# A state space input stored as four wide DRAM writes, and three weight splits moved from VectorE to GpSimd, in a hybrid decoder step

## The chip, the core and the metric

The kernel runs on one core of a Trainium2 chip. A core has a matrix engine (TensorE, called PE in the profile; its weight loads are listed as PEld), three engines for elementwise work (VectorE or DVE, ScalarE or ACT, GpSimd or POOL), and a sequencer (SyncE or SP) whose queue issues the DMA transfers here. Each engine works through its own instructions in order and waits for the others by semaphores. The metric is the device time of one execution in microseconds (us); lower is better.

## What is computed

One layer of a hybrid decoder runs over a prompt of 2048 tokens and 32 sample tokens. Of the input projection `proj = rmsnorm(x) @ w_in` the first 768 columns are q, k, v of a sliding-window attention and the last 512 are `u`, the input of a diagonal state space model (S5) with 32 groups of 16 channels:

```python
q = proj[..., :ATTN_WIDTH]; k = ...; v = ...
u = proj[..., ATTN_WIDTH + 2 * KV_WIDTH:]
attn, k_win, v_win = attend(q, k, v, sinks)
ssm, h_re, h_im = _s5(u, h0_re, h0_im, ...)     # x[t] = a x[t-1] + B u[t];  y[t] = Re(C x[t]) + D u[t]
ssm = gelu(ssm); ssm = ssm * sigmoid(ssm @ w_glu + b_glu)
x = x + concat(rmsnorm(attn), rmsnorm(ssm)) @ w_out
x = x + conv_ffn(rmsnorm(x))
```

The outputs are the two token groups after a final rmsnorm, the last window of keys and values, the last S5 states and the last convolution rows.

## The kernel before

**Split products.** Every large matrix product is made from three: a weight is split into a high part (a rounded copy, made on ACT at L83) and a low part (the raw weight less the high part, L84, on an engine that the caller names), the activations likewise, and `mm3` (L89 to L91) adds high x high, high x low and low x high. `load_split_w` does this for the weights: a DMA into a raw tile (L146), then `split`. The raw tiles share two buffers, so a third raw tile is loaded only when the low part of the first has been made.

**First pass, u.** Tokens are taken in eight tiles (the first of 288 columns, the others of 256). For each, PE makes four products of 128 features (`u`), and DVE scales each into `uperm[m]` (L763), a tile of 128 partitions x 8 steps x 272 columns: partition 16 g + h is channel h of group g of feature tile m, time is cut into 8 steps within a column. Beside this pass DVE and POOL compute the tables of the state space model (`s5_params`): powers of the step factor, `bb1` and `bb2`, and two tables of phases, `fine` and `coarse`, on POOL.

**Between the passes.** The three tiles 1, 2, 3 of q weights are split with the low part on DVE (L781); the loads of token tile 1 follow (`prep2(1)`); then `uperm` goes to the DRAM scratch `uscr[group, 128, 272]`, one store for each of 32 groups (L787), in which 16 partitions are written so that row 16 s + h of a group holds step s of channel h.

**Second pass.** An order written out by hand (`ORDER`) mixes the generators: `q` is one of six 128-column products of a token tile (in the order v, k, then q 0 to 3), `a0` a step of attention block 0, `s0` a step of state space pair 0. It begins `s0 q q q q q q s0 q q s0 q s1 a0 ...`. PE follows this order strictly. The instructions of the other engines and of SP's queue are placed by a planner, which takes what is ready by its own model of time and, among what is ready, what comes first in the program; `tc.high_priority(offset=n)` moves a block n places forward in that precedence. A product is cleared from one of two PSUM buffers by DVE (L879 for q, L886 for k and v) into `f`, which has two buffers too; the low part of q is made on POOL, that of k on DVE (L84), and the `kp` tiles are zeroed (L830 to L837) and copied (L900) on POOL.

**A state space pair** (`s5_pair`) loads `u` for two groups from `uscr` (L385); DVE builds `vv`, an operator whose rows are (s, h) (L393 to L395), and `cl`; PE transposes `vv` (L403) and multiplies `cl` (L405) into `pk`; ACT copies that into `wk`; eight small DMAs place shifted copies of a 16-row piece into `tp`, 16 partitions each (L418). The next step multiplies `wk` with `u` (`pre`, `pim`, L442), DVE scans, and the last one multiplies `tp` with `u` and `cl` with the states into the output, which goes to `yscr`.

Of the kernel before, what the change touches and what calls it, by code (L numbers as in the profile page):

```python
# [9 lines left out]
F32 = mybir.dt.float32  # L10
# [3 lines left out]
ALU = mybir.AluOpType  # L14
# [4 lines left out]
P = 128  # L19
# [6 lines left out]
KD = D // P  # L26
# [36 lines left out]
HPD = 90  # L63
# [17 lines left out]
def split(nc, hi, lo, src, hi_eng, lo_eng):  # L81

    i = nc.scalar.copy(hi, src) if hi_eng is nc.scalar else hi_eng.tensor_copy(hi, src)  # L83
    return i.ins, lo_eng.tensor_tensor(lo, src, hi.bitcast(F32), ALU.subtract).ins  # L84
# [52 lines left out]
def load_split_w(c, pool, raw_pool, src, nk, cols, nm, lo_eng=None, hi_eng=None):  # L137

    nc = c.nc
    v = src.rearrange("(k p) n -> p k n", p=P)  # L140
    out = {}
    for m in cols:
        hi = pool.tile([P, nk, P], F32R, tag=f"{nm}h{m}", name=f"{nm}h{m}")
        lo = pool.tile([P, nk, P], F32R, tag=f"{nm}l{m}", name=f"{nm}l{m}")
        raw = raw_pool.tile([P, KD, P], F32, tag="wur", name=f"{nm}raw{m}")[:, 0:nk]
        nc.sync.dma_start(raw, v[:, :, m * P : m * P + P])  # L146
        split(nc, hi, lo, raw, hi_eng or nc.scalar, lo_eng or nc.gpsimd)
        out[m] = (hi, lo)
    return out
# [229 lines left out]
def s5_pair(c, pool, ps, gp, uscr, yscr):  # L379

    nc, v, gq = c.nc, c.nc.vector, c.nc.gpsimd
    gs = slice(2 * gp, 2 * gp + 2)
    nm = f"s{gp}"
# [3 lines left out]

    cl = pool.tile([P, 2, 9, 16], F32, tag="cl", name=f"cl_{nm}", bufs=2)
    ct = pool.tile([P, 2, 9, 16], F32, tag="ct", name=f"ct_{nm}")
    vv = pool.tile([P, 2, 8, 16], F32, tag="vv", name=f"vv_{nm}")  # L390
    pw = lambda x, n: x[:, gs, 0:n].unsqueeze(3).broadcast_to((P, 2, n, 16))
    hb = lambda x, n: x[:, gs, :].unsqueeze(2).broadcast_to((P, 2, n, 16))
    v.tensor_tensor(vv, pw(c.prv[0], 8), hb(c.bb1, 8), ALU.mult)  # L393
    v.tensor_tensor(ct[:, :, 0:8], pw(c.prv[1], 8), hb(c.bb2, 8), ALU.mult)
    v.tensor_tensor(vv, vv, ct[:, :, 0:8], ALU.add)  # L395
    v.tensor_tensor(cl, pw(c.pr, 9), hb(c.sc1, 9), ALU.mult)
    v.tensor_tensor(ct, pw(c.pi, 9), hb(c.c2, 9), ALU.mult)
    v.tensor_tensor(cl, cl, ct, ALU.subtract)
# [1 line left out]

    pk = ps.tile([P, 512], F32, tag="w", name=f"pk_{nm}")
    for g in range(2):
        nc.tensor.transpose(pk[:, g * P : g * P + P], vv[:, g].rearrange("p s h -> p (s h)"), c.ident)  # L403
    for g in range(2):
        nc.tensor.matmul(pk[0:16, 256 + g * P : 256 + g * P + P], c.bb1[:, 2 * gp + g, :],  # L405
                         cl[:, g, 0:8].rearrange("p t h -> p (t h)"), start=True, stop=True)
    wk = pool.tile([P, 4, P], F32, tag="wk", name=f"wk_{nm}")
# [6 lines left out]
    tp = pool.tile([P, 2, P], F32, tag="tp", name=f"tp_{nm}", bufs=2)  # L414
    gq.memset(tp, 0.0)
    for s in range(8):
        w = 16 * (8 - s)
        nc.sync.dma_start(tp[16 * s : 16 * s + 16, :, P - w : P], wk[0:16, 2:4, 0:w])  # L418
    yield 0.8


# [34 lines left out]
    x = pool.tile([P, 2, NC], F32, tag="x", name=f"x_{nm}")  # L456
# [182 lines left out]
def body(tc, a):  # L639
    nc = tc.nc  # L640
    c = Ctx()
    c.nc, c.tc, c.a = nc, tc, a

    def pool(name, side, bufs=1):
        p = tc.tile_pool(name=name, bufs=bufs, side=side, reuse_waits="tile")
        return p.__enter__(), lambda: p.__exit__(None, None, None)
# [9 lines left out]
    with ExitStack() as top:  # L656
        top.enter_context(tc.manual_schedule(engines={mybir.EngineType.PE}))
        dram = top.enter_context(tc.tile_pool(name="scr", bufs=1, space=DRAM))
        uscr = dram.tile([NG, P, CU], F32, tag="uscr", name="uscr")
# [35 lines left out]
        raw, raw_close = pool("raw1", "left", 2)  # L695
# [12 lines left out]
        uperm = [p1u.tile([P, 8, CU], F32, tag=f"up{m}", name=f"up{m}") for m in (3, 2, 1, 0)][::-1]  # L708
        wu, wq = {}, {}
# [16 lines left out]
        def prep2(it):  # L726
            t0, n = TILES[it]
            xs = load_x(t0, n, f"2_{it}")
            tiles, lo = lo_tiles(xh, n, f"p2_{it}")
            for k, t in enumerate(tiles):  # L730
                nc.sync.dma_start(t.bitcast(F32), loscr[:, 2 * k : 2 * k + 2, t0 : t0 + n])
            return list(zip(scaled_hi(c, xh, xs, g_mix, n, f"p2_{it}"), lo))
# [45 lines left out]
            pass  # L778
        p1w_close()
        wqb, wqb_close = pool("wqb", "right")  # L780
        wq.update(load_split_w(c, wqb, raw, a["w_qkv"], KD, (1, 2, 3), "wq", nc.vector))  # L781
        later = None
        for m in (0, 3, 2, 1):
            if m == UPRE:
                later = prep2(1)
            for g in range(8):
                nc.sync.dma_start(uscr[8 * m + g].rearrange("(s h) c -> h s c", h=16), uperm[m][16 * g : 16 * g + 16])  # L787
        pst_close()
        ps_close()
        p1u_close()  # L790
# [35 lines left out]
        for i in range(2):  # L826
            kp = [kvp.tile([P, 2, 384], F32R, tag=f"kp{i}{j}", name=f"kp{i}{j}") for j in range(2)]
            for t in kp:
                f = t.bitcast(F32)
# [217 lines left out]
        def samples():  # L1047
# [4 lines left out]
            for i, _ in enumerate(g):  # L1052
# [3 lines left out]
                yield  # L1056

        steps = {f"s{i}": s5_pair(c, s5p, PS, i, uscr, yscr) for i in range(NPAIR)}
        steps.update(q=qkv_steps(), e=gelus(), x=samples())
        for tok in ORDER.split():  # L1060
# [154 lines left out]
        hb = xp = psv = hb_close = xp_close = psv_close = None  # L1215
# [436 lines left out]
```

## Time and profile before

| | |
|---|---|
| median of 3 runs | 2220.59 us (2218.52 to 2222.08) |
| profiled execution | 2218.95 us, of which its span 2217.2 us |
| mean granted TensorE clock | 0.969 |
| PE busy in the span | 2055.2 us |
| DVE, ACT, POOL busy | 1323.1, 1054.1, 1200.4 us |
| moved by DMA | 347.59 MB, mean 157 GB/s |

The profile comes from one profiled execution. A row of instructions gives the start in us from the span's start, the duration, the engine, the line of the code, and the tiles written and read; merged rows carry a count (x4) and, in brackets, how long the engine stood idle before and what ended that. A row of a group gives the shortest, median and longest duration in ns. A row of a wait says which line waited for what: us in total, number of times, longest. A row of DMA issues gives the size of each and the median us from issue to landing. A row of a stretch gives PE, PEld, DVE, ACT and POOL busy, each with its count, then the granted clock as a share of full speed, the mean busy share of the 16 DMA engines and the GB/s. SPq is the issuing of a transfer on SP's queue, not the transfer itself.

### The profile page before, as it was taken

The page shows a single profiled execution, that of the slowest core. Times are in us where ns is not written, and L with a number is a line of the kernel's source. Part 1 is how long each engine was busy: PE and PEld are TensorE (multiplying, and loading weights), DVE is VectorE, ACT ScalarE, POOL GpSimd, SP SyncE. Part 2 cuts the span into 40 slices and gives each one's busy share as a digit, 9 for nine tenths or more (in the row PEclk, how much of TensorE's full clock was granted, in tenths as well). Part 3 has the DMA queues.
Part 4 walks back from the last instruction along what each step waited for, and adds up shares of the span by engine and source line. Part 5 has one row for each costly group of instructions (what it writes and reads, how often), then busy time and mean ns, then how long its engine had stood idle before and what let it go on. Part 6 is the DMA issues. An engine that isn't in the chain of part 4 may idle for free.

```text
span 2217.2 us, 41459 instructions
## 1 busy us (share of the span) xinstructions
PE 2055.2 (93%) x14685; PEld 1926.3 (87%) x14685; DVE 1323.1 (60%) x3310; ACT 1054.1 (48%) x2459; POOL 1200.4 (54%) x1184
## 2 busy tenths in 40 slices
PE   8969999978998889999999898999999999799997
PEld 8957878857998889999999686789999999788997
DVE  8859898358566766766666165227766666601231
ACT  6525564675443356666666233225655665602111
POOL 4857776334455466666665453446666666822211
PEclk9979999989999999999999899999999999999999
DMA  7865434686478733333333795834323333573643
GB/s 230 255 149 157 123 107 130 128 232 189 147 236 255 236 125 117 108 96 110 108 107 102 248 284 177 292 130 152 112 93 110 106 101 102 175 191 118 206 131 98
DMA packets 294352, 347.59 MB, mean 157 GB/s; under 512 B 42344, under 2 KB 250864, under 8 KB 294128
## 3 DMA queue, kind: packets, MB, share of 16 engines
q1 hardware_dynamic: 294144, 344.94, 51.5%
q8 instruction: 116, 1.90, 0.4%
q14 instruction: 92, 0.75, 0.1%
HBM read 232.70 MB, written 107.80 MB: 154 GB/s over the span
## 4 chain that ended last, share of the span: by engine, by line
PE 70%; DVE 10%; DMA 7%; POOL 4%; issue 4%; ACT 3%; SPq 2%; DVEq 0%; POOLq 0%; ACTq 0%
PE ux L1345 20%; PE u L1345 16%; PE dn L90 7%; PE dn L91 7%; PE dn L89 6%; DVE xo L1427 1%; PE wo L90 1%; PE wo L91 1%; PE wo L89 1%; PE qkv L89 1%; DMA y<-yscr 1%; PE qkv L91 1%; PE qkv L90 1%; DMA al<-actscr 1%; SPq L787 1%
## 5 line engine op out<-in xcount | busy, mean ns | idle before, releaser
L84 POOL TENSOR_TENSOR wdl<-wdr,wdh 128x1024 fp32r<-128x1024 f32 x65 | 159.0, 2451 | 301.9 <-ACT wdh L83 295.2
L89 PE MATMUL dn<-ah,wdh 128*128 128x512 f32 (+3 forms) x552 | 205.7, 373 | 17.1 <-DMA ah<-actscr 14.1
L91 PE MATMUL dn<-ah,wdl 128*128 128x512 f32 (+3 forms) x552 | 205.8, 373 | 3.3 <-POOL wdl L84 3.3
L90 PE MATMUL dn<-al,wdh 128*128 128x512 f32 (+3 forms) x552 | 205.5, 372 | 1.8 <-DMA al<-actscr 1.7
L1310 ACT ACTIVATE cc<-u,cw 128x260 f32<-128x260 f32 (+1 forms) x252 | 141.5, 563 | 95.1 <-DVE u L1388 67.0
L83 ACT CAST wdh<-wdr 128x1024 fp32r<-128x1024 f32 x65 | 68.0, 1050 | 243.8 <-PE dn L90 210.6
L1502 DVE TENSOR_TENSOR xo<-xo,dn 128x512 f32<-128x512 f32 (+3 forms) x40 | 21.9, 584 | 269.7 <-PE dn L91 269.6
L84 POOL TENSOR_TENSOR wls<-s,whs 128x1024 fp32r<-128x1024 f32 x42 | 101.2, 2409 | 133.9 <-ACT whs L83 133.8
L1311 DVE SCALAR_TENSOR_TENSOR cc<-u,cw,cc 128x260 f32<-128x260 f32 (+1 forms) x252 | 120.8, 480 | 67.8 <-ACT cc L1310 66.2
L89 PE MATMUL wo<-mh,wo 128*128 128x260 f32 x512 | 149.8, 293 | 2.9 <-ACT mh L83 2.0
L90 PE MATMUL wo<-ml,wo 128*128 128x260 f32 x512 | 147.8, 289 | 3.7 <-POOL ml L84 3.6
L91 PE MATMUL wo<-mh,wo 128*128 128x260 f32 x512 | 147.1, 287 | 0.0
L89 PEld LDWEIGHTS dn<-ah,wdh 128*128 128x128 f32 x552 | 105.6, 191 | 35.4 <-DMA ah<-actscr 10.3
L1388 DVE TENSOR_TENSOR u<-u,cb 128x262 f32<-128x262 f32 x84 | 36.4, 434 | 157.3 <-PE u L1345 157.3
L89 PE MATMUL qkv<-hh_p,wqh 128*128 128x256 f32 (+1 forms) x384 | 114.7, 299 | 13.6 <-DVE vs L890 8.5
L91 PEld LDWEIGHTS dn<-ah,wdl 128*128 128x128 f32 x552 | 105.5, 191 | 20.9 <-POOL wdl L84 4.2
L90 PEld LDWEIGHTS dn<-al,wdh 128*128 128x128 f32 x552 | 105.4, 191 | 19.8 <-DMA al<-actscr 2.9
L84 POOL TENSOR_TENSOR wlt<-s,wht 128x512 fp32r<-128x512 f32 x42 | 54.2, 1289 | 122.5 <-ACT wht L83 58.0
L1312 DVE SCALAR_TENSOR_TENSOR cc<-u,cw,cc 128x260 f32<-128x260 f32 (+1 forms) x252 | 119.2, 474 | 0.8
L84 POOL TENSOR_TENSOR wlg<-wur,whg 128x1024 fp32r<-128x1024 f32 x42 | 101.6, 2419 | 28.1 <-ACT whg L83 28.1
L89 PE MATMUL dn<-ah,wd 128*128 128x448 f32 (+2 forms) x288 | 95.0, 330 | 23.0 <-DMA ah<-actscr 19.3
L90 PE MATMUL qkv<-hl_p,wqh 128*128 128x256 f32 (+1 forms) x384 | 111.1, 289 | 0.0
(569 smaller groups left out, 8351.1 us busy)
## 6 DMA issues: line engine op xcount, KB each, us to landing
actscr<-cc SPq DMA_DIRECT2D x168, 260.0 KB, 4.7
wur<-in_w_up SPq DMA_DIRECT2D x84, 512.0 KB, 4.6
wdr<-in_w_down SPq DMA_DIRECT2D x77, 512.0 KB, 4.7
x<-in_xT SPq DMA_DIRECT2D x56, 256.0 KB, 4.3
hs<-h2scr SPq DMA_DIRECT2D x44, 262.0 KB, 4.9
ah<-actscr SPq DMA_DIRECT2D x42, 256.0 KB, 3.9
al<-actscr SPq DMA_DIRECT2D x42, 256.0 KB, 4.4
mt<-mscr SPq DMA_DIRECT2D x16, 520.0 KB, 5.4
```

The costliest lines, as they stand in the source:

```text
L83: i = nc.scalar.copy(hi, src) if hi_eng is nc.scalar else hi_eng.tensor_copy(hi, src)
L84: return i.ins, lo_eng.tensor_tensor(lo, src, hi.bitcast(F32), ALU.subtract).ins
L89: nc.tensor.matmul(ps, w[0], x[0], start=first, stop=False)
L90: nc.tensor.matmul(ps, w[0], x[1], start=False, stop=False)
L91: nc.tensor.matmul(ps, w[1], x[0], start=False, stop=last)
L787: nc.sync.dma_start(uscr[8 * m + g].rearrange("(s h) c -> h s c", h=16), uperm[m][16 * g : 16 * g + 16])
L1310: nc.scalar.activation(cp, pp[:, 2:], AF.Identity, bias=w[3], scale=w[2])
L1311: nc.vector.scalar_tensor_tensor(cp, pp[:, 1 : npr + 1], w[1], cp, ALU.mult, ALU.add)
L1312: nc.vector.scalar_tensor_tensor(cp, pp[:, 0:npr], w[0], cp, ALU.mult, ALU.add)
L1345: nc.tensor.matmul(pt[:, :W], x[p][:, k], y[q][:, k], start=start and k + i == 0, stop=k == 3 and i == 2, skip_group_check=True)
L1388: v.tensor_tensor(c21[s], c21[s], cb[s][:, 0], ALU.add)
L1427: nc.vector.scalar_tensor_tensor(x, x, g_fin[:, k : k + 1], r, ALU.mult, ALU.mult)
```

## The change

Three things are edited.

- `uscr` keeps its shape, but row 8 h + s of a group now holds step s of channel h, so a feature tile is stored by one DMA of 128 partitions instead of eight of 16.
- `s5_pair` follows: `vv` is built as (h, s) instead of (s, h), with the temporary `cv` in the storage of `ct`, and the eight stores into `tp` go to partitions s, s + 8, s + 16, ... instead of 16 adjoining ones.
- The low parts of q weight tiles 1, 2, 3 are made on GpSimd (the default of `load_split_w`) instead of VectorE, and this block is given precedence by `HPD` = 90 places.

```diff
-    vv = pool.tile([P, 2, 8, 16], F32, tag="vv", name=f"vv_{nm}")
+    vv = pool.tile([P, 2, 16, 8], F32, tag="vv", name=f"vv_{nm}")
+    cv = ct.rearrange("p g t h -> p g (t h)")[:, :, 0:P].rearrange("p g (h s) -> p g h s", s=8)
+    pwv = lambda x: x[:, gs, :].unsqueeze(2).broadcast_to((P, 2, 16, 8))
+    hbv = lambda x: x[:, gs, :].unsqueeze(3).broadcast_to((P, 2, 16, 8))
...
-    v.tensor_tensor(vv, pw(c.prv[0], 8), hb(c.bb1, 8), ALU.mult)
-    v.tensor_tensor(ct[:, :, 0:8], pw(c.prv[1], 8), hb(c.bb2, 8), ALU.mult)
-    v.tensor_tensor(vv, vv, ct[:, :, 0:8], ALU.add)
+    v.tensor_tensor(vv, pwv(c.prv[0]), hbv(c.bb1), ALU.mult)
+    v.tensor_tensor(cv, pwv(c.prv[1]), hbv(c.bb2), ALU.mult)
+    v.tensor_tensor(vv, vv, cv, ALU.add)
...
-        nc.tensor.transpose(pk[:, g * P : g * P + P], vv[:, g].rearrange("p s h -> p (s h)"), c.ident)
+        nc.tensor.transpose(pk[:, g * P : g * P + P], vv[:, g].rearrange("p h s -> p (h s)"), c.ident)
...
-        nc.sync.dma_start(tp[16 * s : 16 * s + 16, :, P - w : P], wk[0:16, 2:4, 0:w])
+        nc.sync.dma_start(tp[s:P:8, :, P - w : P], wk[0:16, 2:4, 0:w])
...
-        wq.update(load_split_w(c, wqb, raw, a["w_qkv"], KD, (1, 2, 3), "wq", nc.vector))
+        with tc.high_priority(offset=HPD):
+            wq.update(load_split_w(c, wqb, raw, a["w_qkv"], KD, (1, 2, 3), "wq"))
...
-            for g in range(8):
-                nc.sync.dma_start(uscr[8 * m + g].rearrange("(s h) c -> h s c", h=16), uperm[m][16 * g : 16 * g + 16])
+            nc.sync.dma_start(uscr[8 * m : 8 * m + 8].rearrange("g (h s) c -> (g h) s c", s=8), uperm[m])
```

## The prediction, made before the changed kernel was run

> **What bounds the kernel now.** I read the page first. PE is busy for 2055.2 of 2217.2 us, so what this change can win lies where PE stands still. The page's slices show PE thin in two early places, and a table of 5 us stretches finds them: 120 to 128 us and 150 to 161 us.
>
> ```profile
> span 2217.2 us, 41459 instructions
> PE 2055.2 (93%) x14685; PEld 1926.3 (87%) x14685; DVE 1323.1 (60%) x3310; ACT 1054.1 (48%) x2459; POOL 1200.4 (54%) x1184
> ```
> ```profile
> 105.00:110.00 5.00, 5.00 (x43) 4.95 (x42) 1.55 (x4) 0.90 (x3) 4.67 (x20) 1.00 1.07 349
> ...
> 120.00:125.00 5.00, 0.34 (x3) 0.10 (x1) 5.00 (x1) 0.00 (x0) 5.00 (x9) 0.76 0.00 0
> ...
> 130.00:135.00 5.00, 5.00 (x30) 5.00 (x30) 2.51 (x6) 2.19 (x5) 2.55 (x6) 0.72 1.00 282
> ...
> 140.00:145.00 5.00, 5.00 (x39) 4.60 (x38) 3.20 (x9) 0.41 (x1) 3.93 (x10) 1.00 0.89 196
> ...
> 155.00:160.00 5.00, 0.00 (x0) 0.00 (x0) 1.23 (x4) 1.73 (x5) 0.72 (x1) 0.50 0.95 295
> ```
>
> Columns: PE, PEld, DVE, ACT, POOL busy with counts, granted clock, DMA share, GB/s. From 120 to 125 one DVE instruction fills the stretch and the DMA moves nothing. Next the waits of PE and of SP's queue, and the chain of waits through this place:
>
> ```profile
> PE pre_s L442 <- DMA u_s<-uscr: 11.1, 1, 11.1
> PE qkv L89 <- DVE vs L890: 8.5, 1, 8.5
> SPq L146 <- DVE wql L84: 14.5, 1, 14.5
> ```
> ```profile
> 115.31 11.85 DVE wql L84
> 127.18 0.37 SPq L146
> ...
> 154.98 0.43 SPq L385
> 155.46 6.32 DMA r<-rscr
> ```
>
> So one instruction causes both holes. The low part of the first of the three weight tiles takes 11.85 us. Behind it DVE cannot clear the PSUM of the v and k products (PE's 8.5 us), and the third raw tile cannot be loaded, because it takes the buffer which that low part still reads. On SP's queue the 31 remaining stores of the state space input stand behind that load, and behind the stores stand the loads of u (PE's 11.1 us) and r.
>
> **Why 11.85 us.** Here are the same line elsewhere, and POOL around it:
>
> ```profile
> L84 DVE TENSOR_TENSOR wql<-wqraw,wqh x6: 1210/1222/11844, 62.1 to 132.4; 128x1024 fp32r<-128x1024 f32 x6
> ```
> ```profile
> 115.60 0.60 POOL L192 TENSOR_TENSOR n_co<-coarse 128x256 f32<-128x256 f32 x1
> ...
> 121.78 1.25 POOL L333 TENSOR_TENSOR bb<-bb,bbt 128x512 f32<-128x512 f32 x1
> ...
> 125.62 0.44 POOL L185 TENSOR_TENSOR h<-c_h,c_h 128x128 f32<-128x128 f32 x1
> 126.12 0.41 POOL L830 MEMSET kp<- 64x384 f32 x1
> ...
> 130.27 0.20 POOL L837 MEMSET vtok_z<- 128x128 f32 x1
> 132.69 2.27 POOL L900 CAST kp<-kp 64x128 fp32r<-64x128 f32 x4 [2.23 <-ACT kp L83]
> ```
>
> It normally takes 1.22 us. POOL ran 16 instructions without a gap from 115.60 to 126.06; then came a memset, which reads nothing, and DVE was done 1.1 us later (127.16). I read it as DVE kept from reading its second SBUF input for as long as POOL kept reading. The Trainium skill (SBUF — State Buffer, Who interferes with whom) has the same lock, but says the later instruction blocks until the first finishes: by that, one POOL instruction, at most 1.28 us here. The trace agrees in kind and not in length.
>
> **The change part by part.**
>
> *Low parts to POOL.* DVE loses three instructions, with them the 11.85 us. POOL gains three of the kind in the first row below; the raw load and the cast on ACT are the other two steps of the third tile:
>
> ```profile
> L84 POOL TENSOR_TENSOR wlv<-wur,whv x42: 2378/2395/2945, 749.1 to 1897.2; 128x1024 fp32r<-128x1024 f32 x42
> ```
> ```profile
> L83 ACT CAST wqh<-wqraw x6: 1032/1041/1051, 56.1 to 131.3; 128x1024 fp32r<-128x1024 f32 x6
> ```
> ```profile
> wqraw<-in_w_qkv SPq DMA_DIRECT2D x6, 512.0 KB, 4.6
> ```
>
> That is 3 x 2.40 = 7.2 us more on an engine that is full until 130.5 us. Where in POOL's order they land is the main unknown: the first cast ends only at 115.3, where DVE's low part starts today, and the raised precedence only helps among work that is ready. The bounds are: ahead of the tables (first low part at 115.3), after them (126.1), after the memsets too (130.5). I take the middle. Low parts then end at 128.5 and 130.9; the third raw load goes out at 128.5, lands at 133.5 (0.4 issue, 4.6 landing), is cast by 134.5, and its low part ends at 136.9.
>
> Now PE's order, which is fixed by hand:
>
> ```profile
> 113.70 0.37 PE L89 MATMUL qkv<-hh_p,wqh 128*128 128x288 f32 x1 [0.77 <-DVE up L763]
> ...
> 120.04 0.29 PE L91 MATMUL qkv<-hh_p,wql 128*128 128x288 f32 x1
> 128.87 0.58 PE L89 MATMUL qkv<-hh_p,wqh 128*128 128x288 f32 x1 [8.53 <-DVE vs L890]
> ...
> 143.72 0.38 PE L403 MATMUL pk_s<-ident,vv_s 128*128 128x128 f32 x2
> 144.03 0.61 PE L405 MATMUL pk_s<-cl_s,bb 128*16 128x128 f32 x4
> 161.57 1.18 PE L442 MATMUL pre_s<-u_s,wk_s 128*64 128x272 f32 x4 [11.07 <-DMA u_s<-uscr]
> ```
>
> Two products of the first token tile took 113.70 to 120.33, so 3.2 to 3.3 us each; those of the next tile have 256 of 288 columns, by that 2.85 us. Free of waits, PE has from 120.3 on four products (12.8), the v transposes (0.4), pk (0.9) and two products (5.7), and would be at pre at 140.1 instead of 161.57. The most that can be won is therefore 21.5 us. With the low parts as above: first product of q 120.3 to 123.5, the second waits for its low part, 128.5 to 131.7, the third until 134.9, the fourth waits for 136.9 and ends at 139.9, then pk and two products: pre at 146.5.
>
> POOL gives some of this back. The copy f of each q product has two buffers, and POOL's low part of q frees them; before, that already cost DVE a little:
>
> ```profile
> 143.99 0.42 DVE L879 SCALAR_TENSOR_TENSOR f<-qkv,r 128x256 f32<-128x256 f32 x1 [1.50 <-POOL q L84]
> ```
>
> If memsets (4.4 us) and kp casts (2.3 us) come after 136.9, the first q low part ends near 144.5, and the two products of the next tile go out only as DVE clears PSUM: pre at 150.6. If the memsets fit into the wait for the third cast (130.9 to 134.5): 146.5. I take 148.5. DVE's low part of k, also with two SBUF inputs, can be locked out until POOL's next gap, by the trace up to 130.9; PE waits for low parts until 128.5 anyway, so this costs under 1 us. By the page's rule it would cost nothing.
>
> *The stores.* Now 32 stores with 1088-byte runs from 16 partitions each, 31 of them here:
>
> ```profile
> 110.36 0.34 SPq L787 DMA_DIRECT2D uscr<-up  x1
> 110.79 1.82 SPq L731 DMA_DIRECT2D hl_p<-loscr  x3
> 127.18 0.37 SPq L146 DMA_DIRECT2D wqraw<-in_w_qkv  x1
> 127.64 0.54 SPq L731 DMA_DIRECT2D hl_p<-loscr  x1
> 128.23 23.27 SPq L787 DMA_DIRECT2D uscr<-up  x31
> ```
> ```profile
> uscr<-up SPq DMA_DIRECT2D x32, 136.0 KB, 3.5
> ```
>
> 32 x 136 KiB is 4.46 MB; 31 of 32 parts in 23.27 us is 186 GB/s, at a DMA share of 0.89. In the new layout a partition's eight steps follow each other in DRAM, so each feature tile is one store of 128 partitions with 8704-byte runs. No row shows such a store. The nearest with wide transfers are the stretches at 349 and 282 GB/s, so 3.2 to 3.95 us for each 1.11 MB; upward the bound is today's 6 us. I take 3.9. SP's own time falls from 32 issues to 4. The first store, which holds what the first u load reads, keeps its place at 110.4. The other three are ready when DVE has cleared the last u product, just before PE's 113.70; either they go ahead of the third raw load (done by 126) or behind it: 129.5 + 3 x 3.9 = 141.2, then the 3.4 us of other issues up to the u load (row at 154.98, stores' end at 151.5), and at most the 6.3 us that r took: 150.9. Ahead, PE's own 148.5 sets pre's start; behind, 150.9 does. I take 149.6, between the two, and 161.57 - 149.6 is 12 us.
>
> r of the next token tile has one buffer and cannot be loaded before the last q product is cleared (144 to 147 in the new order); its landing near 150 fits, it is no new term.
>
> *The operator's new order.* Three DVE products per pair keep their 256 elements; such lines with and without broadcast operands differ by under 0.03 us (0.417 against 0.394), so 48 instructions are bounded by 1.4 us either way; I take 0. The eight small stores into tp per pair go to every eighth partition instead of 16 adjoining ones, with the same number of runs:
>
> ```profile
> L394 DVE TENSOR_TENSOR ct_s<-prv,bb x16: 360/417/984, 138.3 to 367.3; 128x256 f32<-128x256 f32 x16
> L461 DVE TENSOR_TENSOR a_s<-x_s,er_s x16: 390/394/630, 168.2 to 386.5; 128x256 f32<-128x256 f32 x16
> ```
> ```profile
> 194.60 3.27 DMA tp_s<-wk_s
> ```
>
> That landing is on the chain once; half or double would be -1.6 or +3.3 us. I take 0.
>
> *Sum.* -12 us at pre, and what follows waits for no fixed time, so it all moves with it, on an engine that is busy for 93% of the span. The profiled execution took 2218.95 us, its span and 1.75 us around it, 1.64 us under the median of 2220.59. Against it the sum gives 2207, against the median 2208.6. I forecast 2208. A measurement of this kernel can tell about 0.2% (4.4 us) from nothing.
>
> **The rivals.**
>
> *Nearly all is won* (gain 16 to 21.5, 2199 to 2204). POOL takes the low parts as the casts end, at 115.3, and the stores stand ahead of the third load. For it: the code gives these instructions precedence over the last tables. Against it: bb, which pk needs, would end 4.8 to 7.2 us after 123.0, and POOL still owes memsets and q low parts. Chance 0.2.
>
> *POOL and SP take over as the bound* (gain 0 to 6, 2215 to 2220). The first low part comes after the memsets, ending at 132.9, later than DVE's 127.16; the last one, by the same steps, at 141.3; the fourth product ends at 144.3, where it ends now, and the stores stand behind the third load: 134 + 11.7 + 3.4 + 6.3 = 155.4, and pre 6 us early, less whatever q's low parts cost on POOL. For it: POOL's rows are full without a gap, and the present order has the raw load ahead of 31 stores. Against it: the first store alone already carries the first pairs. Chance 0.2.
>
> *Slower* (about 2226). The same lateness, but the stores run no faster than now, because it is DRAM writes and not the runs that limit them. Then 133.0 for the third load instead of 127.18, +5.8 us on the chain with everything behind it. It decides from the point at which four stores take over 17.5 us (23.3 less 5.8), under 255 GB/s. For it: the share is already 0.89 during the stores. Against it: 349 GB/s with stores among the traffic. Chance 0.09.
>
> **How the numbers follow.** Forecast (gain 7 to 16) 0.51, nearly all 0.2, new bound 0.2, slower 0.09. Of the new-bound case six parts in ten lie within 4.4 us of the median; so faster 0.78, same 0.13, slower 0.09. The range reaches from the full 21.5 us with 1 us of the small terms (2198) to a gain of under 2 us (2219).
>
> **What would show it.** After: no wql on DVE; no DVE instruction near 11 us, or one at kp low parts; PE's 8.5 us wait replaced by a shorter one on POOL's wql; four uscr stores with over 280 GB/s; pre at 146 to 151 us. I am wrong if POOL's first low part starts after 130 us, if the stores show under 255 GB/s, or if PE waits longer for q's PSUM behind POOL than it did for u.

## The result, and the profile after

The changed kernel took 2211.98 us (median of 10 runs, 2203.21 to 2218.23) against 2221.64 us for the kernel before in the same measurement (10 runs): a ratio of 0.9947, 95% interval 0.9933 to 0.9962. It is 9.7 us faster; the forecast was 2208, 4 us below what came. The profiled execution took 2211.34 us at a mean granted clock of 0.971 (before 0.969).

The first two lines of the page after, as those of before were shown:

```profile
span 2209.6 us, 41415 instructions
...
PE 2056.0 (93%) x14685; PEld 1926.6 (87%) x14685; DVE 1319.1 (60%) x3307; ACT 1053.2 (48%) x2459; POOL 1209.4 (55%) x1187
```

PE has the same work and the span is 7.6 us shorter, so all of it is waits. The waits of the kernel after from 100 to 175 us:

```profile
PE qkv L91 <- POOL wql L84: 5.7, 1, 5.7
...
PE qkv L89 <- DVE qs L885: 3.4, 1, 3.4
```

The wait of 11.1 us for u is gone. The wait of 8.5 us for DVE has become two, 5.7 and 3.4 us, which is 9.1 us. PE's own rows, the ends of the waits and the first state space step:

```profile
113.97 0.37 PE L89 MATMUL qkv<-hh_p,wqh 128*128 128x288 f32 x1 [0.78 <-DVE up L766]
...
129.96 0.61 PE L91 MATMUL qkv<-hh_p,wql 128*128 128x288 f32 x1 [5.69 <-POOL wql L84]
...
138.98 0.58 PE L89 MATMUL qkv<-hh_p,wqh 128*128 128x288 f32 x1 [3.38 <-DVE qs L885]
...
153.65 0.68 PE L445 MATMUL pre_s<-u_s,wk_s 128*64 128x272 f32 x4
```

`pre`, at 161.57 before, now starts at 153.65, 7.9 us earlier, and the last row has no bracket: it did not wait for u. What SP's queue did in the place of its 23.27 us of stores:

```profile
110.63 0.34 SPq L790 DMA_DIRECT2D uscr<-up  x1
...
129.93 0.37 SPq L146 DMA_DIRECT2D wqraw<-in_w_qkv  x1
130.40 0.54 SPq L734 DMA_DIRECT2D hl_p<-loscr  x1
131.03 2.00 SPq L790 DMA_DIRECT2D uscr<-up  x3
...
143.28 0.43 SPq L385 DMA_DIRECT2D u_s<-uscr  x1
```

The third raw load goes out 2.8 us later than before (127.18), and yet the load of u, at 154.98 before, goes out at 143.28. The 5 us stretches in which the stores move (columns as in the prediction; GB/s is the last one, the granted clock the third from the end):

```profile
130.00:135.00 5.00, 5.00 (x21) 5.00 (x22) 0.00 (x0) 1.00 (x2) 4.70 (x9) 0.50 0.75 251
135.00:140.00 5.00, 1.62 (x7) 1.30 (x7) 4.48 (x9) 1.97 (x7) 4.56 (x7) 0.84 1.02 430
```

And the place of the new second wait, in the rows of POOL, ACT and DVE:

```profile
125.37 0.46 POOL L185 TENSOR_TENSOR h<-c_h,c_h 128x128 f32<-128x128 f32 x1
125.88 0.41 POOL L833 MEMSET kp<- 64x384 f32 x1
...
127.57 4.70 POOL L84 TENSOR_TENSOR wql<-wqraw,wqh 128x1024 fp32r<-128x1024 f32 x2
...
135.12 2.35 POOL L84 TENSOR_TENSOR wql<-wqraw,wqh 128x1024 fp32r<-128x1024 f32 x1 [0.26 <-ACT wqh L83]
```
```profile
134.00 1.04 ACT L83 CAST wqh<-wqraw 128x1024 fp32r<-128x1024 f32 x1 [17.16 <-DMA wqraw<-in_w_qkv]
134.95 0.83 ACT L83 CAST kp<-f 64x256 fp32r<-64x256 f32 x2
```
```profile
135.38 2.83 DVE L84 TENSOR_TENSOR kp<-f,kp 64x256 fp32r<-64x256 f32 x2 [14.24 <-ACT kp L83]
138.31 0.42 DVE L882 SCALAR_TENSOR_TENSOR f<-qkv,r 128x256 f32<-128x256 f32 x1
138.65 0.18 DVE L885 SCALAR_TENSOR_TENSOR qs<-qkv,r 128x32 f32<-128x32 f32 x1
```

Read from the bottom: PE's product at 138.98 waits for DVE to clear the first q product (138.31 to 138.83). DVE does that only after its low parts of k, for which it stood idle 14.24 us, waiting for ACT's high parts of k. These stand on ACT behind the cast of the third weight tile, which waited for its raw load until 134.00, and that load had waited on SP for the buffer which POOL's first low part reads until 129.91. When DVE's first low part of k could start at last, it met POOL's third low part (135.12 to 137.47) and took 2.37 us instead of 0.43.

### The profile page after: what moved, and what is told of

Its sections match the earlier page's. It is cut to its first block, busy times and chain, and to the rows that moved or that the text cites. A ratio compares the mean times of both kernels' runs of the same rounds, so it can differ in the third digit from the quotient of the medians.

```text
span 2209.6 us, 41415 instructions
## 1 busy us (share of the span) xinstructions
PE 2056.0 (93%) x14685; PEld 1926.6 (87%) x14685; DVE 1319.1 (60%) x3307; ACT 1053.2 (48%) x2459; POOL 1209.4 (55%) x1187
## 4 chain that ended last, share of the span: by engine, by line
PE 70%; DVE 8%; DMA 7%; POOL 7%; issue 4%; ACT 3%; SPq 1%; DVEq 0%; POOLq 0%; ACTq 0%
PE ux L1348 20%; PE u L1348 16%; PE dn L90 7%; PE dn L91 7%; PE dn L89 7%; PE qkv L89 2%; PE qkv L91 2%; PE qkv L90 2%; DVE xo L1430 1%; DMA y<-yscr 1%; PE o L555 1%; PE tp_b L544 1%; POOL ml L84 1%; PE wo L89 1%; PE wo L91 1%
## 5 line engine op out<-in xcount | busy, mean ns | idle before, releaser
L91 PE MATMUL qkv<-hh_p,wql 128*128 128x256 f32 (+1 forms) x384 | 111.5, 290 | 5.7 <-POOL wql L84 5.7
```

Source lines behind the costliest of these rows:

```text
L91: nc.tensor.matmul(ps, w[1], x[0], start=False, stop=last)
```

## The experiments

All medians, with the ratio to the kernel before in the same measurement; `pre` is the start of the first state space step in the profiled execution (before 161.57, after 153.65). The numbers of lines shift by one to three between these kernels.

| run | what it is | us | ratio, 95% interval | `pre` |
|---|---|---|---|---|
| e1_stores | stores and operator alone | 2206.66 | 0.9939, 0.9917 to 0.9960 | 149.83 |
| e2_pool | low parts on POOL alone | 2222.70 | 1.0011, 0.9995 to 1.0027 | 163.51 |
| e8_narrow | after, stores in 16 partitions | 2224.87 | one run | 162.25 |
| e4_memset | before, a memset in POOL's tables | 2218.81 | 0.9991, 0.9976 to 1.0005 | 156.48 |
| e7_after_kp | after, k's low part on POOL | 2214.03 | 0.9959, 0.9944 to 0.9974 | 155.12 |
| e11_third_cast | after, third cast on POOL | 2211.82 | 0.9941, 0.9924 to 0.9958 | 150.14 |
| e5_after_raw3 | after, three raw buffers | 2219.80 | 0.9997, 0.9981 to 1.0013 | 150.97 |
| e6_stores_raw3 | stores, three raw buffers | 2215.45 | 0.9970, 0.9956 to 0.9985 | 149.72 |
| e10_stores_memset_raw3 | the same, and the memset | 2216.06 | 0.9970, 0.9957 to 0.9984 | 151.08 |
| e12_raw3_r | e6 with r's load raised | 2207.61 | 0.9922, 0.9901 to 0.9943 | 150.02 |
| e14_all_r | e10 with r's load raised | 2210.78 | 0.9944, 0.9929 to 0.9958 | 148.44 |
| e9_stores_memset | stores and the memset | 2204.85 | 0.9915, 0.9899 to 0.9931 | 146.84 |

### One part of the change at a time

e1_stores leaves the low parts on DVE, without the raised precedence:

```diff
-        with tc.high_priority(offset=HPD):
-            wq.update(load_split_w(c, wqb, raw, a["w_qkv"], KD, (1, 2, 3), "wq"))
+        wq.update(load_split_w(c, wqb, raw, a["w_qkv"], KD, (1, 2, 3), "wq", nc.vector))
```

> Only the stores and the operator's new order; the three low parts stay on VectorE. Theory A (the stores carry the gain, the move of the low parts gives some of it back): VectorE's low part still takes about 11.8 us and PE still waits about 8.5 us for it, but three wide stores leave SP's queue in some 2 us instead of 22, u and r are there early, and pre starts when PE gets to it, near 150.5 us where it got to it before; 11 us gained, ratio about 0.995, as fast as the full change or up to 3 us faster. Theory B (the prediction's emphasis: the freed VectorE brings most of it): pre not before 157, gain under 5 us.

e2_pool is the kernel before with only the two lines marked "-" above put in the place of the one marked "+".

> Only the low parts on GpSimd with the precedence; 32 narrow stores as before. Theory A: the third raw load waits for GpSimd's low part until about 129.9 us instead of 127.2, 31 stores in 23 us stand behind it, pre starts near 164; 2 to 3 us slower than before, ratio about 1.001. Theory B: VectorE and PE are free from 120 us on, pre starts before 158, ratio under 0.998.

Measured: the stores alone 0.9939, the low parts alone 1.0011 with 1 inside the interval. Of the stores alone, PE's wait, its `pre`, and the group of DVE's low parts (count, then shortest, median, longest in ns):

```profile
128.57 0.58 PE L89 MATMUL qkv<-hh_p,wqh 128*128 128x288 f32 x1 [8.55 <-DVE vs L892]
...
149.83 0.68 PE L445 MATMUL pre_s<-u_s,wk_s 128*64 128x272 f32 x4
```
```profile
L84 DVE TENSOR_TENSOR wql<-wqraw,wqh x6: 1211/1222/12133, 61.7 to 132.0; 128x1024 fp32r<-128x1024 f32 x6
```

Of the low parts alone, SP's stores and `pre`:

```profile
130.79 22.89 SPq L788 DMA_DIRECT2D uscr<-up  x31
```
```profile
163.51 1.18 PE L442 MATMUL pre_s<-u_s,wk_s 128*64 128x272 f32 x4 [10.14 <-DMA u_s<-uscr]
```

With the stores alone DVE still takes 12.1 us over one low part and PE still waits 8.55 us, and yet `pre` comes 11.7 us earlier than before: the wait for u is gone and nothing replaces it. With the low parts alone the raw load goes out later, 31 stores stand behind it as ever, and `pre` comes 1.9 us later than before. So the stores carry the gain. Joined to them, the low parts on POOL set `pre` back by 3.8 us (153.65 against 149.83); the two times, 0.9947 and 0.9939, have overlapping intervals and do not resolve that.

The raised precedence was not run by itself. Built without it, the changed program keeps the order of PE, DVE, ACT and POOL; only two small loads of the initial states stand earlier on SP's queue.

### Which property of the stores counts

e8_narrow keeps the new layout, with its eight steps of a channel side by side, and the low parts on POOL, but stores each feature tile by eight DMAs of 16 partitions:

```diff
-            nc.sync.dma_start(uscr[8 * m : 8 * m + 8].rearrange("g (h s) c -> (g h) s c", s=8), uperm[m])
+            for g in range(8):
+                nc.sync.dma_start(uscr[8 * m + g].rearrange("(h s) c -> h s c", s=8), uperm[m][16 * g : 16 * g + 16])
```

> The changed kernel, the new layout in DRAM, but stored as 32 stores of 16 partitions each, with 8704-byte runs. Tells apart what made the stores fast. If it is the length of the runs, 24 to 31 stores move at 300 GB/s or more and take 11 to 14 us. If it is the 128 partitions of one store, they stay near 190 GB/s, 18 to 23 us, and pre starts near 160 us or later.

SP's rows and one stretch of the stores:

```profile
131.14 19.69 SPq L791 DMA_DIRECT2D uscr<-up  x31
```
```profile
140.00:145.00 5.00, 5.00 (x24) 5.00 (x24) 1.79 (x3) 0.00 (x0) 5.00 (x10) 0.55 0.93 218
```

31 x 136 KiB in 19.69 us is 219 GB/s; with 1088-byte runs it was 186 before. The eightfold run brings 18%. The rest, up to the stretch at 430 GB/s of the kernel after, came with stores of 128 partitions instead of 16, which also means 3 transfers at this place instead of 31. That SP's issuing of so many is the limit is not what the records of the DMA engines say: with the engines busy for 0.93 of the time, a packet of 8704 bytes took a median of 529 ns in e8 (the shortest 328) and of 328 ns in the kernel after. The transfers themselves were slower; what made them so is open. At 219 GB/s the stores are still on the path (`pre` at 162.25, with 7.44 us of waiting for u).

### What holds DVE's low part

e4_memset is the kernel before with one instruction more in `renorm`, which writes a tile that is free by then and changes no value (the planner also moves some of POOL's table instructions then):

```diff
     v.tensor_tensor(t1, t1, t2, ALU.add)
+    v.memset(t2, 0.0)
     v.tensor_scalar(t1, t1, -0.5, 1.5, ALU.mult, ALU.add)
```

> The kernel before, with one more instruction on GpSimd for each renormalisation: a memset of its scratch tile t2, after the sum that reads it; the result is unchanged. The last of them falls between the tables near 118 to 120 us. If VectorE is shut out only while GpSimd reads without a break, the first low part ends within about 2.5 us of that memset, near 120 us instead of 127.2; PE's 8.5 us wait shrinks to about 1; the third load and the 31 stores go out some 7 us earlier; pre near 154 to 155, 6 to 7 us gained, ratio about 0.997. If the 11.8 us has another cause (a data wait that ends when the tables end), it stays at 11 us or more and the time does not change.

POOL at that place, and the group of DVE's low parts in the same kernel:

```profile
120.70 1.06 POOL L333 TENSOR_TENSOR bbt<-b,ff 128x512 f32<-128x512 f32 x1
121.69 0.31 POOL L195 MEMSET n_co<- 128x256 f32 x1
```
```profile
L84 DVE TENSOR_TENSOR wql<-wqraw,wqh x6: 1216/1414/5564, 62.9 to 128.2; 128x1024 fp32r<-128x1024 f32 x6
```

The longest low part started at 117.27 and took 5.56 us instead of 11.84: it ended at 122.83, 0.83 us after the memset, with POOL's reading instructions going on to 130. One instruction that reads nothing, in a run of others that read, let DVE through. From the start of POOL's memset to the end of the held low part it is 1.0 us in the kernel before and in e1, where the memset comes behind POOL's tables, and 1.1 us here and in e9 (below), where it comes among them; that bears out the reading of the prediction for these runs. PE's wait for DVE fell to 2.37 us, not to the 1 us expected. `pre` came 5.1 us earlier, though the first pass ended 2.9 us later here; the time, 0.9991 where 0.997 was expected, does not resolve it.

### What makes the second wait

e7_after_kp moves the low part of k to POOL:

```diff
-                        split(nc, kp[0][rr, kv, P:384], kp[1][rr, kv, P:384], f[rr, :], nc.scalar, nc.vector)
+                        split(nc, kp[0][rr, kv, P:384], kp[1][rr, kv, P:384], f[rr, :], nc.scalar, nc.gpsimd)
```

> The changed kernel with the low part of k on GpSimd instead of VectorE. In the trace after, VectorE waits 14.2 us for the cast of k and then takes 2.83 us for two low parts, and only then clears the first q product. Theory A: VectorE clears it at about 124 us, so PE's second wait (3.4 us) goes and PE is held only by the low parts of the q weights (132.3, 137.5); pre near 149 to 151, 3 to 4 us faster than the changed kernel, unless GpSimd's added work (16 low parts of k, some 0.8 us each) holds back f and takes it away. If the low part of k on VectorE costs nothing, pre stays at 153 to 154.

This was a miss. POOL is in order as well: k's low parts come at 137.50 and 138.53, behind the third weight tile's, and PE's second wait grew to 4.98 us (`pre` at 155.12). What had to go was the queue on ACT. e11_third_cast makes the high part of the third tile on POOL; in the built program one instruction changes its engine and no other its place:

```diff
-            wq.update(load_split_w(c, wqb, raw, a["w_qkv"], KD, (1, 2, 3), "wq"))
+            for m in (1, 2, 3): wq.update(load_split_w(c, wqb, raw, a["w_qkv"], KD, (m,), "wq", None, nc.gpsimd if m == 3 else None))
```

> After, with the high part of the third weight tile on GpSimd instead of ACT; built, this changes one instruction's engine and no other instruction's place. Theory (k's cast stands behind the third cast on ACT, and that is PE's second wait): k's cast leaves ACT near 121.5 us instead of 135, DVE's kp low part ends by 133 instead of 138.2, and PE's 3.4 us wait on DVE's qs is gone. In its place PE can wait for the third low part, which stands behind a cast on POOL of 1.2 to 3.3 us: it ends at 138.5 to 140.6 us, pre at 152.6 to 154.7 us, time within 3 us of the changed kernel's 2212. Rival (DVE is held by POOL's reads whatever ACT does): the kp low part still ends after 137 us and PE's wait on DVE's qs is 3 us or longer.

ACT, then DVE, then PE of this kernel:

```profile
125.83 0.83 ACT L83 CAST kp<-f 64x256 fp32r<-64x256 f32 x2 [9.78 <-POOL h L185]
```
```profile
126.26 0.87 DVE L84 TENSOR_TENSOR kp<-f,kp 64x256 fp32r<-64x256 f32 x2 [5.21 <-ACT kp L83]
127.24 0.42 DVE L882 SCALAR_TENSOR_TENSOR f<-qkv,r 128x256 f32<-128x256 f32 x1
```
```profile
130.00 0.61 PE L91 MATMUL qkv<-hh_p,wql 128*128 128x288 f32 x1 [5.83 <-POOL wql L84]
...
138.51 0.40 PE L91 MATMUL qkv<-hh_p,wql 128*128 128x288 f32 x1 [0.31 <-POOL wql L84]
```

The clearing that ended the 3.4 us wait is done at 127.76 instead of 138.83, and that wait is gone; in its place stand 0.31 us for POOL and 1.8 us for DVE's `cl` at the transposes, and `pre` is at 150.14, earlier than the theory's range. So the queue on ACT was the cause. Two things in the expectation were wrong: k's cast left at 125.83, not 121.5, because it also waits for the last of POOL's tables, and POOL's own cast took 1.04 us, less than the bound of 1.2. The 3.5 us are not seen in the time, 0.9941 against 0.9947; behind `pre`, at 174 us, PE waits for `cl` once more, for 1.79 us, which the kernel after does not.

### Three raw buffers, and where their gain went

If the third raw load need not wait for the first low part, nothing on SP or ACT stands behind it. The same edit was made to the kernel after (e5) and to the stores alone (e6), and to the latter with the memset (e10):

```diff
-        raw, raw_close = pool("raw1", "left", 2)
+        raw, raw_close = pool("raw1", "left", 3)
```

> The changed kernel with three raw buffers instead of two, so that the third raw tile is loaded beside the other two, far ahead. Theory A with the wait found in the trace after (ScalarE stands 17 us before the third cast, and behind it in its order stands the cast of k, behind that VectorE's low part of k, behind that the clearing of PSUM): these three waits go. The first low part still starts near 127.6 us, so PE still waits about 5.7 us for it; then the other products follow without a wait, pre near 147 to 148; 6 us faster than the changed kernel, ratio to before about 0.993. If the third load is not what holds ScalarE and VectorE, pre stays at 153 to 154 and the ratio at that of the change.

> The stores alone with three raw buffers; low parts on VectorE. Theory A: all three low parts stand in front of the clearing of v, the first is shut out until about 127.2 us and the others follow until 129.6; the stores leave at 114 us. Nothing is won over the stores alone, since PE waits for VectorE in either: pre near 150 to 152, ratio to before about 0.995. If the third load were what counts in that kernel too, pre would come at 145 or earlier.

> The stores, three raw buffers, low parts on VectorE, and the memset of e4_memset. If the lock opens at a write-only instruction of GpSimd, at least the first low part ends near 120 us, and the following ones find the lock between two GpSimd instructions or wait until the next write near 126 us. All through at 120: PE has no wait, pre near 141 to 143, 19 us gained, ratio 0.991. Only the first through: VectorE clears v near 128.5, pre near 149, ratio 0.995.

The load goes out early and the three stores leave at 116.3 (e5), 117.0 (e6) and 119.6 us (e10), but none of the three ratios expected (0.993, 0.995, and 0.991 or 0.995) came. The times are worse than without the third buffer: 0.9997 against 0.9947 for the kernel after, whose intervals do not meet, and 0.9970 against 0.9939 for the stores alone, whose intervals just do.

The expectations of e6 and e10 also had DVE's first low part held by POOL's reads. It was not: no low part took over 1.24 us in e6 and 1.29 in e10, and e6 has no memset there. DVE and POOL in e6:

```profile
116.28 3.52 DVE L84 TENSOR_TENSOR wql<-wqraw,wqh 128x1024 fp32r<-128x1024 f32 x3 [1.61 <-ACT wqh L83]
```
```profile
116.32 1.26 POOL L197 TENSOR_TENSOR ws16i<-ws16i,n_ws 128x16 f32<-128x16 f32 x1
117.53 1.20 POOL L205 COPY coarse<-ws16r 128x16 f32<-128x16 f32 x1
```

In this build the planner has POOL's tables later, and the low parts fall among instructions of 16 columns (32 in e10), which took 0.21 to 0.22 us in the kernel before. Here it was POOL that was held, three times for the length of a low part. So not every run of reads keeps DVE out; what decides who gets in first, no run separates. It also means that e10 did not test its memset.

Two things were found for the lost time. First, in e6 the cast of k leaves ACT at 132.23, when the last of POOL's tables is done (in this build at 132.2 instead of 125.8), and PE's wait is 6.3 us: POOL's tables are the next bound right behind the raw load. Second, the gain that is left at `pre` is lost after it. SP in e6, and PE's wait (e10 has the same 5.0 us, and e5 6.7 us):

```profile
145.39 5.63 SPq L421 DMA_DIRECT2D tp_s<-wk_s  x8
151.06 0.58 SPq L851 DMA_DIRECT2D r<-rscr  x1
```
```profile
PE qkv L89 <- DVE f L888: 5.0, 1, 5.0
```

The load of r for the second token tile stands behind the eight small stores into `tp`; with two raw buffers it stands ahead of them. Without r DVE cannot clear that tile's products. e12_raw3_r raises the precedence of r's loads in e6 (which moves the loads of some other tiles a few places too, and some DVE instructions behind them):

```diff
-            nc.sync.dma_start(r, rscr[:, t0 : t0 + n].broadcast_to((P, n)))
+            with tc.high_priority(offset=HPD): nc.sync.dma_start(r, rscr[:, t0 : t0 + n].broadcast_to((P, n)))
```

> The stores alone with three raw buffers (2215.5 us), and the load of the next r raised in precedence, so that it stands ahead of the eight small tp stores on SP's queue instead of behind them. Theory (with three raw buffers the gain at pre was lost because r's load stood behind these stores): r leaves near 145.5 us instead of 151.1, PE's 5.0 us wait for the clearing of the next tile's first product falls under 1 us, and the time falls by 4 to 6 us to 2209 to 2212. Rival (the loss has another place): the r load moves and the wait goes, but the time stays at 2214 to 2217 us.

SP in e12, then the stretch from 150 to 200 us of e6 and of e12:

```profile
145.00 0.34 SPq L851 DMA_DIRECT2D r<-rscr  x1
145.51 5.58 SPq L421 DMA_DIRECT2D tp_s<-wk_s  x8
```
```profile
150.00:200.00 50.00, 43.69 (x310) 36.66 (x307) 42.66 (x142) 23.48 (x80) 29.52 (x57) 0.93 0.47 133
```
```profile
150.00:200.00 50.00, 48.31 (x353) 39.39 (x353) 48.79 (x159) 25.17 (x83) 34.48 (x64) 1.00 0.53 152
```

`pre` is where it was, the 5.0 us wait is gone, PE is busy 4.6 us more in the 50 us after it, and the ratio falls from 0.9970 to 0.9922, with intervals that do not meet. e14_all_r does the same to e10:

> New layout and four stores, low parts on DVE, one memset among POOL's tables, three raw buffers, and the load of r raised in precedence. Theory: r's load ahead of the tp stores gives back what the same kernel without that lost (2216.1): time 2208 to 2212 us; the first pass still ends 3 to 4 us later than with the stores alone, so it does not beat these (2206.7). Rival (the r load was not what cost): 2214 to 2218 us.

It came out at 0.9944 against 0.9970, as that theory has it, with intervals that just touch. So the order on SP's queue, with what moved along with r, accounts for the whole loss of e6 against the stores alone (0.9922 beside 0.9939), and for about half of that of e10 against the same kernel with two buffers (e9 below, 0.9915). In e5 it was not tested.

### Stores and memset together

e9_stores_memset has the new stores, the low parts on DVE, two raw buffers, and the memset among POOL's tables.

> Before with the new layout and its four stores, the low parts left on DVE, two raw buffers, and one memset of a free table tile among POOL's tables (the memset changes no value). Theory (POOL's unbroken run of reads holds DVE, and the third raw load waits for that low part): the longest wql low part falls from 12.1 us to about 5.6 us, the third raw load leaves near 123 us, PE's 8.5 us wait falls to 2 to 5 us, and because the load of r keeps its place ahead of the eight small tp stores, most of that arrives at the end: pre at 145 to 150 us, time 2203 to 2207 us, no slower than with the stores alone (2206.7). Rival (PE's wait there is made up by something else later, as with the third raw buffer): time 2212 to 2218 us.

SP's raw load, PE's wait and `pre`, and SP's load of r with the `tp` stores behind it:

```profile
121.55 0.37 SPq L146 DMA_DIRECT2D wqraw<-in_w_qkv  x1
...
140.94 0.33 SPq L852 DMA_DIRECT2D r<-rscr  x1
...
144.25 5.90 SPq L422 DMA_DIRECT2D tp_s<-wk_s  x8
```
```profile
124.30 0.58 PE L89 MATMUL qkv<-hh_p,wqh 128*128 128x288 f32 x1 [4.33 <-DVE vs L893]
...
146.84 0.68 PE L446 MATMUL pre_s<-u_s,wk_s 128*64 128x272 f32 x4
```

The wait on DVE is halved, `pre` is the earliest of all, and r keeps its place. The ratio to before is 0.9915 (0.9899 to 0.9931); the changed kernel's was 0.9947 (0.9933 to 0.9962). The two were not timed in one measurement, but their intervals against the same kernel do not meet. Against the stores alone (0.9939, 0.9917 to 0.9960) they overlap, so that the memset adds to these is not resolved.

## Why the prediction was right, and where it was not

**The cause.** Right: one DVE low part, held by POOL's reads, stood behind both holes. The memset shows the holding, and e1 and e2 show that the two holes are separate ways to the end: the change had to mend the second, the path through SP's stores, to gain anything. The prediction took the freed DVE as part of the gain; with the 12.1 us low part still there, e1's `pre` is at 149.83, earlier than that of the change.

**The stores.** The direction was right and the size too careful. 3.9 us each (some 285 GB/s) was taken from the stretches at 349 and 282; the new stores ran in a stretch at 430 GB/s. The load of u went out at 143.28 and took 2.9 us (median of the 16 such loads), so it was there 7 us ahead of `pre`. It went out only 1.3 us before the 144.6 of the prediction, as the other transfers between the stores and it took 10.2 us on SP instead of 3.4; the larger part is its landing, 2.9 us where up to 6.3 had been allowed. The prediction's second way, 150.9 through u, was never the later one. The prediction named the longer runs and the 128 partitions together; by e8 the runs are the smaller part.

**The low parts.** Their price (2.40 us; 2.35 measured) and their place (127.57 where 126.1 had been taken, as five memsets went first) were near. The step that failed is the sum of PE's order from there to `pre`, 146.5 to 150.6 with 148.5 taken, against 153.65. Three of its terms were off:

- "DVE's low part of k ... costs under 1 us". That step looked at DVE and POOL, and not at what k's high part is queued behind on ACT. That is the third cast, and with the raw load 2.8 us later than before, k's low part came late and into POOL's third low part. PE's next product started 3.6 us after the one before it (3.4 of it counted as waiting), and e11 takes that away. (Before, the cast of k stood behind the third one too, at 132.22, and cost nothing, as PE had begun its first q product only at 128.87.)
- "3.2 to 3.3 us each" for a product. It holds for PE at full clock. After each wait the granted clock was half of that for a while (0.50 from 130 to 135 us), and the two products behind the waits were 2.2 and 1.6 us longer than that.
- The first low part was 1.5 us late. The 1.8 us that the prediction had PE wait for the third low part did not come, as PE was late itself.

1.5 + 2.2 + 3.6 + 1.6 - 1.8 is 7.1 us, and the last product of the first tile ended at 146.94 instead of 139.9. From there to `pre` it took 6.7 us, as forecast (6.6). The 2.0 us taken for POOL's low parts of q were not spent: with PE later, they were out of the way. So the 5.1 us between 148.5 and 153.65 are accounted for. That the miss is no larger is in part luck: terms that came 8.9 us late were offset by the 1.8 and 2.0 us that were not needed, and by the 1.1 us added for the stores' way (149.6 instead of 148.5).

**The operator's new order and the `tp` stores** were taken at 0. In the stretch to 400 us the three DVE lines of `vv` sum to 27.4 us in the kernel after and 26.7 before, 0.7 us in 48 instructions, and a `tp` store takes 0.59 us on SP (median of 128) in both. It was not timed alone, but the rows agree with 0.

**The sum.** 12 us at `pre` were forecast and 7.9 came; the 4.1 us are the 4 us between 2208 and 2212. That what is won at `pre` arrives at the end held for this kernel (7.9 and 7.6 us) but is no law, as e6 shows: there the planner's new order put the load of r behind eight stores, and PE lost 5.0 us of it again.

**The rivals.** "Nearly all is won" did not come, as POOL started no low part before its tables were done. "POOL and SP take over as the bound" came in part: POOL's low part is now PE's longest wait there, but the gain was 7.9 and not 0 to 6. The slower case needed more than 17.5 us of stores behind the third load. (The 255 GB/s given for that count four stores; the three that stand behind the load would have to fall under 191.) e8's stores, of 16 partitions, took 19.69 us, and its `pre` is 0.7 us later than before. Whether it is slower is not shown: its one run, 2224.87 us, lies among those of before, 2217.39 to 2229.70.

**What it said would show.** No first-pass wql on DVE, no instruction near 11 us there, the 5.7 us wait on POOL's wql and stores over 280 GB/s were seen; `pre` at 146 to 151 was not. Of the three signs of being wrong none appeared. The chances, by their own parts, come to 0.79 for faster and 0.12 for same, not 0.78 and 0.13.

## What to carry to other kernels

Where a load is given later, list what stands behind its consumer on every engine, not only on the one it was moved to: here the casts on ACT set the second wait. Where a queue's order comes from a planner, look at the places of the other transfers after every edit; one small load behind eight stores made PE wait 5.0 us. Of two edits in one change, time each by itself: here one carried all of the gain.

## What the runs showed of the hardware

- **The hold of DVE by POOL is opened by one instruction that does not read.** 11.84 us fell to 5.56 (e4) and 12.13 to 6.63 (e1 to e9) with a memset of 0.31 us among POOL's reads. The hold goes both ways: beside the low parts of e6 POOL's instructions took 1.20 to 1.26 us instead of 0.21 to 0.22 in the kernel before. The Trainium skill (SBUF — State Buffer, Who interferes with whom) says that a DVE instruction with two SBUF inputs contends with a GpSimd instruction that reads and not with one that only writes; in that, these runs agree.
- **A wait costs more than its length on PE.** Behind the wait of 5.7 us the matmuls of 288 columns started every 0.24 us instead of every 0.13, for 5.4 us, and again for 3.3 us behind the wait of 3.4. Four rows of PE after, the first two at the slow pace, the others at the full one:

```profile
133.00 0.44 PE L91 MATMUL qkv<-hh_p,wql 128*128 128x288 f32 x1
133.24 0.44 PE L89 MATMUL qkv<-hh_p,wqh 128*128 128x288 f32 x1
...
142.67 0.29 PE L90 MATMUL qkv<-hl_p,wqh 128*128 128x288 f32 x1
142.81 0.29 PE L91 MATMUL qkv<-hh_p,wql 128*128 128x288 f32 x1
```

  The granted clock in the stretch from 130 to 135 us was 0.50. The Trainium skill (TensorE: Matmul & The Clock Gate, What's actually happening) has half the clock after an idle window of some 3.4 us, until a busy one has passed; these rows agree.
- **Stores from 16 partitions ran at 186 to 219 GB/s, those from 128 in a stretch at 430**, though the 16 DMA engines showed a busy share of 0.89 and 0.93 with the slow ones. A high busy share did not say that the transfers were at their limit: the same packet of 8704 bytes took 529 ns with 16 partitions and 328 with 128.
